# A hybrid decoder step on one core: groups of the down projection, order of the output projection's second half, and place of the gating functions

## The chip, the cores and the metric

The kernel runs on one core of one Trainium2 chip. The core has TensorE (PE, matmuls; PEld is its weight load), VectorE (DVE), ScalarE (ACT), GpSimd (POOL) and SyncE (SP), which issues most transfers. Each engine works off its own instruction stream in order; streams meet through semaphores. The metric is the device time of one execution in microseconds; less is better.

## The reference, cut to what matters

Two layers over 1024 prompt tokens and 8 decode tokens, 1032 columns in all, model width 1024, float32.

```python
mod = silu(c) @ w_ada + b_ada                       # shift1, scale1, gate1, shift2, scale2, gate2
h = rmsnorm(x, g_norm1) * (1 + scale1) + shift1
z, xbc, dt_raw, cq, ckv, kpe, u = split(h @ w_in)   # 384, 896, 6, 256, 128, 32, 256 columns
xbc = silu(causal_conv(xbc, conv_w, conv_b))        # x (384), B (256), C (256) of the scan
y = chunked_ssd_scan(x, dt, A, B, C)                # chunks of 128 tokens, decays exp(...)
ssd_out = rmsnorm((y + d_skip * x) * silu(z))       # two groups
mla_out = rmsnorm(latent_attention(...))            # 8 decode tokens read 64 pages each
pool_out = pool_mixer(u)
x = x + gate1 * (concat(ssd_out, mla_out, pool_out) @ w_out)
h2 = rmsnorm(x, g_norm2) * (1 + scale2) + shift2
x = x + gate2 * ((silu(h2 @ w_gate) * (h2 @ w_up)) @ w_down)   # FFN width 2816
```

## The kernel before

Activations lie transposed: 128 features on the partitions, the 1032 tokens along the free axis. Every large product is made from three matmuls on split operands: a value is cast to a short form (`wh`, `ac`, `op`, `X`; ScalarE, line 88) and the remainder (`wl` and the like) is the value less the cast one (line 93 on GpSimd in pieces of 129 columns, line 95 on VectorE); `mm3` (lines 139 to 141) adds high x high, low x high and high x low. A framework puts each engine's stream in order at compile time, by program order and by when it expects operands; `keep_in_program_order` pins an instruction behind the one written before it on its engine. Tiles come from pools of fixed size: 24 of kind C (`NA`), 20 of kind B (`NBUF`), seven accumulation banks `psd` and `psg`.

A layer goes through these stages.

- Norm, then input projection (`in_proj`): 16 blocks `m` of 128 output columns, three banks each. Each is evicted by VectorE (times the row's reciprocal norm `r`, line 291), the shift's contribution is copied (`sb`, line 292), the 8 decode columns are added (line 293), and ScalarE adds the bias in place (`evac`, line 296). Blocks 6 to 12 go through the causal convolution on VectorE (`conv`, `cv`), 13 to 15 are the gate z. From block 8 on, steps of the other mixers' preparation run in between (`side`): latents, decode queries, softplus, the pool mixer with its evictions `po` (line 436).
- `conv_silu` (line 383): ten Silu of 128x1032 on ScalarE, over the seven convolved blocks and the three of z, pinned behind each other. Then `table()` (line 213) loads ScalarE's function table with Ln and Exp, for all that follows.
- The weave: the chunked scan (decay products L517, matrices `M` L525 and `E`, L554 and L570 on the Silu's results), the latent attention and the decode tokens' pages, step by step in turn.
- Output projection (`out_proj`): two halves g of 516 columns, eight blocks m each. For step i = 8g + m the weight of i + 2 is loaded (`out_load`), that of i + 1 is split (`out_conv`; low part on VectorE for i in `OPV`). Each weight is loaded and split twice, once per half. A block's result times its gate plus the residual goes to `xb` (line 1440), is squared (`sq`, line 1446) and stored. Squares are added up by blocks; the sum over features is a matmul (line 1476), and `norm_half` makes the normalised operands X of one half during the other's products.
- FFN up (`ffn`, first part): 22 blocks f of 128, seven products each, results through Silu to DRAM (`actd`).
- FFN down (second part of `ffn`): the 22 activations go in groups `FFB`; for each group all eight output blocks m are computed, n x 3 x 3 matmuls of 344 columns for a group of n, and added to `x` (`resid`, lines 1356 to 1360, the last an addition over 8 columns on VectorE). An activation is loaded (`ar`) and split (`ac`, low part on GpSimd for even f, on VectorE for odd f) by `fetch`: the first group's before the first block, each later group's one per block from m = 1 of the group before. The weight of step i + 1 is split in step i, its low part on GpSimd.

Of the kernel before, what the change touches and what calls it, by code (L numbers as in the profile page):

```python
# [9 lines left out]
AF = mybir.ActivationFunctionType  # L10
ALU = mybir.AluOpType
# [6 lines left out]
TP = 1024  # L18
# [4 lines left out]
TQ, TQ2 = 258, 516  # L23
# [5 lines left out]
PAST = 8192  # L29
SCALE = 96 ** -0.5  # L30
FF = 22
FFB = (6, 6, 6, 4)
PGW = 258
GP = 16

# [13 lines left out]
class Net:  # L49
# [234 lines left out]
    def evac(self, o, ps, r, func=None):  # L284

        nc = self.nc
        n = T - 2 * TH
        b = self.S([128, 9], "sb", bufs=3)
        for t in range(3):
            a = slice(TH * t, min(TH * t + TH, T))  # L290
            nc.vector.tensor_tensor(out=o[:, a], in0=ps[t][:, :a.stop - a.start], in1=r[:, a], op=ALU.mult)  # L291
        nc.vector.tensor_copy(b, ps[2][:, n:n + 9])
        nc.vector.tensor_tensor(out=o[:, TP:], in0=o[:, TP:], in1=b[:, 1:9], op=ALU.add)
        if func is None:
            return b
        nc.scalar.activation(out=o[:, :TP], in_=o[:, :TP], func=func, bias=b[:, 0:1])

    def sums(self, parts, mix=False):

# [8 lines left out]
    def in_proj(self, l, X, r):  # L308
        nc, A = self.nc, self.A
        out = self.pj = {}  # L310
        raws = {} if l else {2: self.w2}
        W = {}
# [21 lines left out]
        for i, m in enumerate(ORD):  # L334
            if l or i:
                for j in range(1, WSA + 1):
                    prefetch(i + j)
                    conv(i + j)
                prefetch(i + WSA + 1)
            if i in pss:  # L340
                ps = pss.pop(i)
            else:
                ps = self.psum3(TH)
                self.gemm(ps, wk(i), X)
            del W[i]
            t = self.C(name=f"pj{m}")
            self.evac(t, ps, r, AF.Identity)
            out[m] = t
            if 6 <= m < 13:
                out[m] = self.conv(l, m - 6, t)  # L350
            yield
# [25 lines left out]
        nc.sync.dma_start(A["o_sconv"][l, :, c, 2, :], x[:, TP:])  # L377
        return y

    def conv_silu(self):  # L380
        for m in (9, 11, 6, 7, 8, 10, 12, 13, 14, 15):
            y = self.pj[m]
            self.tc.keep_in_program_order(self.nc.scalar.activation(out=y, in_=y, func=AF.Silu))

# [984 lines left out]
            yield  # L1369

    def out_load(self, l, i):
        if i < 16:
            self.oraw[i] = self.load_w(self.A["wout"][l, i % 8], 1024)

    def out_conv(self, i):
        if i < 16:
            self.ow[i] = self.split_w(self.oraw.pop(i), 1024, self.nc.vector if i in OPV else None)

    def out_pre(self, l):
# [15 lines left out]
    def out_proj(self, l, mod, xsrc, side):  # L1395


        nc, A = self.nc, self.A
        todo = [(g, m) for g in range(2) for m in range(8)]
        ms, W = self.ms, self.ow  # L1400
        self.xb, self.acc = [None, None], [None, None]
        for i, (g, m) in enumerate(todo):
            if m == 0:
                xb = self.xb[g] = {(e, j): self.C(name="xb") for e in range(2) for j in range(2)}
                sqs = self.acc[g] = [None, None, None]
            if m % 2 == 0:
                sq2 = self.C(name="sq")
            self.out_load(l, i + 2)
            self.out_conv(i + 1)
            if g:  # L1410
                for _ in range(SDO):
                    next(side[0], None)
            elif m == UF0:
                self.up_first(l)
            elif m > UF0:
                for _ in range(UFN):
                    self.up_ahead(l)
            if i == 1:
# [3 lines left out]
                for _ in self.out_cut(1):  # L1422
                    pass
                self.mx = self.om = None
            if m % 2 == 0:
                xt2 = self.C(name="xt")
            xt = xt2[:, TQ2 * (m % 2):TQ2 * (m % 2) + TQ2]
            nc.sync.dma_start(xt, xsrc(m)[:, TQ2 * g:TQ2 * g + TQ2])
            wh, wl = W.pop(i)
            ps = [self.bank()[:, :TQ] for _ in range(2)]  # L1430
            self.gemm(ps, lambda k: (wh[:, 128 * k:128 * k + 128], wl[:, 128 * k:128 * k + 128]),
                      [[o[:, TQ * j:TQ * j + TQ] for o in ms[g]] for j in range(2)])
            gt = mod[:, 16 + m, :]
            kp, e = divmod(m, 2)
            sq = sq2[:, TQ2 * (m % 2):TQ2 * (m % 2) + TQ2]
            for j in range(2):
                o = xb[e, j][:, TQ * kp:TQ * kp + TQ]
                a = slice(TQ * j, TQ * j + TQ)
# [6 lines left out]
                    nc.vector.tensor_tensor(out=o[:, n:], in0=xt[:, TQ2 - NB:], in1=t, op=ALU.add)  # L1445
                nc.scalar.activation(out=sq[:, a], in_=o, func=AF.Square)
                nc.sync.dma_start(A["xres"][m, :, TQ * (2 * g + j):TQ * (2 * g + j) + TQ], o)
            z = 2 if m == 7 else m % 2
            if sqs[z] is None:
                sqs[z] = sq  # L1450
            else:
                (nc.vector if g or m % 2 else nc.gpsimd).tensor_tensor(out=sqs[z], in0=sqs[z], in1=sq, op=ALU.add)
            if m == 7:
                del ms[g]
                yield

# [280 lines left out]
def build(nc, tc, A):  # L1737
    with tc.tile_pool(name="c", bufs=1) as cp, tc.tile_pool(name="s", bufs=1) as sm, \
# [54 lines left out]
        for l in range(L):  # L1793
# [13 lines left out]
            for m in range(16):  # L1807
                next(pr)
                if l == 0 and 4 + m < ADB[0][0][1]:
                    n.ada(l, mod, 4 + m)  # L1810
                if m >= 8:
                    next(side, None)
                if m == 11:
                    n.kt0 = []
                    for i in range(16):
                        n.smp_gather(l, 0, i, n.kt0)
            for _ in side:
                pass
            del X, r, pr
            n.conv_silu()  # L1820
            n.table()
            n.weave = Weave()
            n.wqk = {}
# [45 lines left out]
SDO = 2  # L1869
LD = 1  # L1870
KSP, SPV, KCV, OGV = (), (), 1, 0
UF0, UFN = 3, 2
WA0, W_L, W_F, W_G = 0, 10, 28, 30
OPO = (6, 7, 0, 1, 2, 3, 4, 5)
XFV, WPF, WPS, OPV = (), (), (), (0, 2, 4, 6, 8, 9, 10, 11, 12, 13, 14, 15)
# [165 lines left out]
```

## Time and profile before

| | |
|---|---|
| median of 3 runs | 3675.45 us (3671.54 to 3679.14) |
| the profiled execution: its time | 3681.19 us |
| its span, first to last instruction | 3679.3 us |
| its mean granted TensorE clock | 0.971 |

The profile is of one execution, which took 3681.19 us; 1.9 us of that lie outside the span. Times in the rows are counted from the span's start. Layer 0 has its input projection from about 68 to 267 us, its weave to about 1030, output projection to about 1148, FFN up to 1604 and FFN down to 1865; layer 1 begins there and has the same stages, the last input eviction at 2088, FFN down from 3416.

### The profile page before, as it was taken

To read this page: it belongs to the slowest core of one execution; us is meant where nothing else is said; L and a number is where in the kernel's file an instruction comes from. 1 tells how busy PE (TensorE), PEld (TensorE's weight loads), DVE (VectorE), ACT (ScalarE), POOL (GpSimd) and SP (SyncE) were. 2 spreads that over 40 slices of the span, in tenths; PEclk is the share of its full clock that TensorE was granted. 3 is DMA by queue.
4 is the path that set the end of the run, shared out by engine and by line. 5 is a ranking of instruction groups with operands and counts; after the bars stand their busy time and mean duration, and the time that the engine had idled before them with its cause. 6 is when DMAs were issued, how large, how long until landed. Compare 5 with 4: busy or idle time off the path is not lost. (4 is left out here: it accounts for less than half of the span.)

```text
span 3679.3 us, 68341 instructions
## 1 busy us (share of the span) xinstructions
PE 3441.4 (94%) x23682; PEld 3069.7 (83%) x23682; DVE 2237.4 (61%) x4328; ACT 1730.5 (47%) x4487; POOL 1867.1 (51%) x3346
## 2 busy tenths in 40 slices
PE   8988999898988999999999889899998889999999
PEld 6976666677887999999999676667777889999999
DVE  4557866767777555552345578767677675555432
ACT  4226566667755333331132456667677453333210
POOL 3336655555440766664433366556464226666642
PEclk9999999999999999999999999999999999999999
DMA  5233655443443222242222346444443522221531
GB/s 198 49 83 122 215 163 163 139 138 114 145 139 100 87 81 79 78 172 86 83 81 56 89 135 225 138 135 123 112 126 114 163 84 87 75 82 70 179 98 70
DMA packets 255336, 430.20 MB, mean 117 GB/s; under 512 B 38736, under 2 KB 180944, under 8 KB 254992
## 3 DMA queue, kind: packets, MB, share of 16 engines
q1 hardware_dynamic: 246800, 409.04, 35.0%
q0 software_dynamic: 8192, 16.79, 1.7%
q8 instruction: 189, 3.10, 0.3%
q14 instruction: 155, 1.27, 0.1%
HBM read 372.84 MB, written 52.87 MB: 116 GB/s over the span
## 5 line engine op out<-in xcount | busy, mean ns | idle before, releaser
L1165 POOL TENSOR_TENSOR lt<-pg,lt 128x128 fp32r<-128x128 f32 x1024 | 436.8, 460 | 465.1 <-ACT lt L1163 393.3
L1182 ACT ACTIVATE sqk<-psd 128x384 f32<-128x384 f32 x1024 | 498.6, 510 | 224.5 <-PE psd L141 152.8
L1329 DVE TENSOR_REDUCE ss<-sqk 128x12 f32<-128x768 f32 x448 | 422.4, 947 | 187.6 <-ACT sqk L1182 177.2
L139 PE MATMUL psd<-mv,lt 128*128 128x390 f32 x1024 | 436.1, 426 | 28.3 <-ACT scr L1183 25.1
L140 PE MATMUL psd<-X,wp 128*128 128x258 f32 x1408 | 398.8, 283 | 4.2 <-DVE wp L95 4.2
L139 PE MATMUL psd<-X,wp 128*128 128x258 f32 x1408 | 399.2, 284 | 3.5 <-ACT wp L88 3.5
L141 PE MATMUL psd<-X,wp 128*128 128x258 f32 x1408 | 398.1, 283 | 0.0
L140 PE MATMUL psd<-mv,lt 128*128 128x390 f32 x1024 | 361.5, 353 | 2.5 <-issue 2.2
L141 PE MATMUL psd<-mv,lt 128*128 128x390 f32 x1024 | 362.2, 354 | 1.1 <-issue 0.7
L93 POOL TENSOR_TENSOR wl<-wr,wh 128x129 fp32r<-128x129 f32 (+1 forms) x312 | 174.7, 598 | 311.6 <-ACT wh L88 244.8
L93 POOL TENSOR_TENSOR wp<-wr,wp 128x129 fp32r<-128x129 f32 x480 | 263.9, 581 | 103.0 <-ACT wp L88 99.1
L1116 POOL DMA_INDIRECT kp<-kpeT,kidx x256 | 260.1, 1016 | 105.4 <-issue 79.6
L140 PE MATMUL psg<-X,wp 128*128 128x258 f32 x1056 | 299.2, 283 | 7.1 <-DVE wp L95 7.1
L139 PEld LDWEIGHTS psd<-mv,lt 128*128 128x128 f32 x1024 | 200.2, 195 | 124.3 <-ACT scr L1183 55.2
L139 PE MATMUL psg<-X,wp 128*128 128x258 f32 x1056 | 299.1, 283 | 2.6 <-ACT wp L88 2.6
L141 PE MATMUL psg<-X,wp 128*128 128x258 f32 x1056 | 298.7, 283 | 0.0
L139 PE MATMUL psd<-op,wh 128*128 128x348 f32 (+1 forms) x792 | 250.9, 318 | 22.9 <-DVE pj L291 10.3
L140 PEld LDWEIGHTS psd<-X,wp 128*128 128x128 f32 x1408 | 267.0, 190 | 5.3 <-DVE wp L95 5.2
L139 PEld LDWEIGHTS psd<-X,wp 128*128 128x128 f32 x1408 | 266.9, 190 | 4.6 <-ACT wp L88 4.6
L141 PEld LDWEIGHTS psd<-X,wp 128*128 128x128 f32 x1408 | 267.0, 190 | 0.0
L140 PE MATMUL psd<-op,wl 128*128 128x348 f32 (+1 forms) x792 | 250.5, 316 | 7.0 <-POOL wl L93 3.5
L141 PE MATMUL psd<-op,wh 128*128 128x348 f32 (+1 forms) x792 | 248.3, 315 | 0.1
(467 smaller groups left out, 9870.3 us busy)
## 6 DMA issues: line engine op xcount, KB each, us to landing
pg<-pages SPq DMA_DIRECT2D x1024, 129.0 KB
wa<-wada SPq DMA_DIRECT2D x96, 512.0 KB
wr<-wff SPq DMA_DIRECT2D x96, 512.0 KB
ar<-actd SPq DMA_DIRECT2D x44, 516.0 KB
actd<-G SPq DMA_DIRECT2D x40, 516.0 KB
wd<-wdn SPq DMA_DIRECT2D x48, 384.0 KB
wr<-win SPq DMA_DIRECT2D x32, 512.0 KB
wr<-wout SPq DMA_DIRECT2D x32, 512.0 KB
```

Source lines behind the costliest of these rows:

```text
L93: nc.gpsimd.tensor_tensor(out=l[:, c], in0=x[:, c], in1=h[:, c].bitcast(F32), op=ALU.subtract)
L139: nc.tensor.matmul(ps, wh, xh, start=start, stop=False)
L140: nc.tensor.matmul(ps, wl, xh, start=False, stop=False)
L141: nc.tensor.matmul(ps, wh, xl, start=False, stop=stop)
L1116: self.nc.gpsimd.indirect_dma_start(out=kts[-1][:, 128 * g:128 * g + 128], out_offset=None, in_=self.A["kpeT"], in_offset=bass.IndirectOff ...
L1165: nc.gpsimd.tensor_tensor(out=ll[:, a], in0=v[:, a], in1=lh[:, a].bitcast(F32), op=ALU.subtract)
L1182: nc.scalar.activation(out=sq, in_=d[:, kc], func=AF.Square)
L1329: nc.vector.tensor_reduce(out=o, in_=x, axis=AX.X, op=ALU.add)
```

## The change

Three edits. The down projection's groups become 4, 6, 6, 6 instead of 6, 6, 6, 4. The output projection's second half goes through the blocks backwards, 7 to 0, and its first `ORE` = 2 blocks (7 and 6) take the split weights of the first half, which are kept for them. And the Silu of blocks 6 to 11 stands in the program behind block 12 of the input projection, that of block 12 behind block 13 (`SIL`), while blocks 13 to 15 are evicted with Silu in place of Identity, with a second Silu over the 8 decode columns, both pinned in program order.

```diff
--- before.py
+++ after.py
@@ -29,7 +29,7 @@
 PAST = 8192
 SCALE = 96 ** -0.5
 FF = 22
-FFB = (6, 6, 6, 4)
+FFB = (4, 6, 6, 6)
 PGW = 258
 GP = 16
 
@@ -293,7 +293,10 @@
         nc.vector.tensor_tensor(out=o[:, TP:], in0=o[:, TP:], in1=b[:, 1:9], op=ALU.add)
         if func is None:
             return b
-        nc.scalar.activation(out=o[:, :TP], in_=o[:, :TP], func=func, bias=b[:, 0:1])
+        keep = self.tc.keep_in_program_order if func == AF.Silu else lambda x: x
+        keep(nc.scalar.activation(out=o[:, :TP], in_=o[:, :TP], func=func, bias=b[:, 0:1]))
+        if func == AF.Silu:
+            keep(nc.scalar.activation(out=o[:, TP:], in_=o[:, TP:], func=func))
 
     def sums(self, parts, mix=False):
 
@@ -344,7 +347,7 @@
                 self.gemm(ps, wk(i), X)
             del W[i]
             t = self.C(name=f"pj{m}")
-            self.evac(t, ps, r, AF.Identity)
+            self.evac(t, ps, r, AF.Silu if m >= 13 else AF.Identity)
             out[m] = t
             if 6 <= m < 13:
                 out[m] = self.conv(l, m - 6, t)
@@ -377,8 +380,8 @@
         nc.sync.dma_start(A["o_sconv"][l, :, c, 2, :], x[:, TP:])
         return y
 
-    def conv_silu(self):
-        for m in (9, 11, 6, 7, 8, 10, 12, 13, 14, 15):
+    def conv_silu(self, ms):
+        for m in ms:
             y = self.pj[m]
             self.tc.keep_in_program_order(self.nc.scalar.activation(out=y, in_=y, func=AF.Silu))
 
@@ -1369,11 +1372,13 @@
             yield
 
     def out_load(self, l, i):
-        if i < 16:
-            self.oraw[i] = self.load_w(self.A["wout"][l, i % 8], 1024)
+        if i < 16 and not 8 <= i < 8 + ORE:
+            self.oraw[i] = self.load_w(self.A["wout"][l, i if i < 8 else 15 - i], 1024)
 
     def out_conv(self, i):
-        if i < 16:
+        if 8 <= i < 8 + ORE:
+            self.ow[i] = self.ow[15 - i]
+        elif i < 16:
             self.ow[i] = self.split_w(self.oraw.pop(i), 1024, self.nc.vector if i in OPV else None)
 
     def out_pre(self, l):
@@ -1396,23 +1401,24 @@
 
 
         nc, A = self.nc, self.A
-        todo = [(g, m) for g in range(2) for m in range(8)]
+
+        todo = [(g, q, 7 - q if g else q) for g in range(2) for q in range(8)]
         ms, W = self.ms, self.ow
         self.xb, self.acc = [None, None], [None, None]
-        for i, (g, m) in enumerate(todo):
-            if m == 0:
+        for i, (g, q, m) in enumerate(todo):
+            if q == 0:
                 xb = self.xb[g] = {(e, j): self.C(name="xb") for e in range(2) for j in range(2)}
                 sqs = self.acc[g] = [None, None, None]
-            if m % 2 == 0:
+            if q % 2 == 0:
                 sq2 = self.C(name="sq")
             self.out_load(l, i + 2)
             self.out_conv(i + 1)
             if g:
                 for _ in range(SDO):
                     next(side[0], None)
-            elif m == UF0:
+            elif q == UF0:
                 self.up_first(l)
-            elif m > UF0:
+            elif q > UF0:
                 for _ in range(UFN):
                     self.up_ahead(l)
             if i == 1:
@@ -1422,17 +1428,19 @@
                 for _ in self.out_cut(1):
                     pass
                 self.mx = self.om = None
-            if m % 2 == 0:
+            if q % 2 == 0:
                 xt2 = self.C(name="xt")
-            xt = xt2[:, TQ2 * (m % 2):TQ2 * (m % 2) + TQ2]
+            xt = xt2[:, TQ2 * (q % 2):TQ2 * (q % 2) + TQ2]
             nc.sync.dma_start(xt, xsrc(m)[:, TQ2 * g:TQ2 * g + TQ2])
-            wh, wl = W.pop(i)
+            wh, wl = W[i] if 8 - ORE <= i < 8 else W.pop(i)
+            if i >= 8:
+                W.pop(15 - i, None)
             ps = [self.bank()[:, :TQ] for _ in range(2)]
             self.gemm(ps, lambda k: (wh[:, 128 * k:128 * k + 128], wl[:, 128 * k:128 * k + 128]),
                       [[o[:, TQ * j:TQ * j + TQ] for o in ms[g]] for j in range(2)])
             gt = mod[:, 16 + m, :]
             kp, e = divmod(m, 2)
-            sq = sq2[:, TQ2 * (m % 2):TQ2 * (m % 2) + TQ2]
+            sq = sq2[:, TQ2 * (q % 2):TQ2 * (q % 2) + TQ2]
             for j in range(2):
                 o = xb[e, j][:, TQ * kp:TQ * kp + TQ]
                 a = slice(TQ * j, TQ * j + TQ)
@@ -1445,12 +1453,12 @@
                     nc.vector.tensor_tensor(out=o[:, n:], in0=xt[:, TQ2 - NB:], in1=t, op=ALU.add)
                 nc.scalar.activation(out=sq[:, a], in_=o, func=AF.Square)
                 nc.sync.dma_start(A["xres"][m, :, TQ * (2 * g + j):TQ * (2 * g + j) + TQ], o)
-            z = 2 if m == 7 else m % 2
+            z = 2 if q == 7 else q % 2
             if sqs[z] is None:
                 sqs[z] = sq
             else:
-                (nc.vector if g or m % 2 else nc.gpsimd).tensor_tensor(out=sqs[z], in0=sqs[z], in1=sq, op=ALU.add)
-            if m == 7:
+                (nc.vector if g or q % 2 else nc.gpsimd).tensor_tensor(out=sqs[z], in0=sqs[z], in1=sq, op=ALU.add)
+            if q == 7:
                 del ms[g]
                 yield
 
@@ -1810,6 +1818,8 @@
                     n.ada(l, mod, 4 + m)
                 if m >= 8:
                     next(side, None)
+                if m in SIL:
+                    n.conv_silu(SIL[m])
                 if m == 11:
                     n.kt0 = []
                     for i in range(16):
@@ -1817,7 +1827,6 @@
             for _ in side:
                 pass
             del X, r, pr
-            n.conv_silu()
             n.table()
             n.weave = Weave()
             n.wqk = {}
@@ -1869,7 +1878,8 @@
 SDO = 2
 LD = 1
 KSP, SPV, KCV, OGV = (), (), 1, 0
-UF0, UFN = 3, 2
+UF0, UFN, ORE = 3, 2, 2
+SIL = {12: (6, 7, 8, 9, 10, 11), 13: (12,)}
 WA0, W_L, W_F, W_G = 0, 10, 28, 30
 OPO = (6, 7, 0, 1, 2, 3, 4, 5)
 XFV, WPF, WPS, OPV = (), (), (), (0, 2, 4, 6, 8, 9, 10, 11, 12, 13, 14, 15)
```

## Rows read from the trace of the kernel before

**Rows 1.** The page, busy time of each engine: us, share of the span, instructions.
```profile
PE 3441.4 (94%) x23682; PEld 3069.7 (83%) x23682; DVE 2237.4 (61%) x4328; ACT 1730.5 (47%) x4487; POOL 1867.1 (51%) x3346
```

**Rows 2.** Windows: busy us (instructions) per engine, granted clock, DMA share, GB/s.
```profile
267.10:280.30 13.20, 5.43 (x25) 3.59 (x21) 1.06 (x4) 13.15 (x17) 0.00 (x0) 0.79 0.75 209
1604.50:1672.00 67.50, 62.30 (x369) 60.49 (x368) 33.33 (x40) 16.61 (x18) 44.88 (x97) 0.95 0.57 200
1800.00:1860.00 60.00, 60.00 (x383) 60.00 (x382) 26.52 (x66) 15.88 (x21) 20.60 (x39) 1.00 0.24 86
2089.40:2102.50 13.10, 5.47 (x25) 3.59 (x21) 1.11 (x4) 13.05 (x17) 0.00 (x0) 0.81 0.70 192
```

**Rows 3.** Timeline of ScalarE behind layer 0's last eviction: start, us, instruction [idle before].
```profile
266.00 1.15 ACT L296 ACTIVATE pj<-pj,sb 128x1024 f32<-128x1024 f32 x1 [0.25 <-DVE sb L292]
267.17 1.28 ACT L383 ACT_TABLE_LOAD   x1
268.46 6.78 ACT L383 ACTIVATE cv<-cv 128x1032 f32<-128x1032 f32 x7
275.15 2.95 ACT L383 ACTIVATE pj<-pj 128x1032 f32<-128x1032 f32 x3
278.11 1.28 ACT L213 ACT_TABLE_LOAD   x1
279.40 0.89 ACT L525 ACTIVATE M<-psg,nat 128x128 f32<-128x128 f32 x3
```

**Rows 4.** Timeline of TensorE, same place.
```profile
280.34 2.93 PE L517 MATMUL psg<-acr,kt 128*128 128x128 f32 x12 [3.04 <-ACT M L525]
```

**Rows 5.** Timeline of ScalarE, end of the output projection's first half, layer 0.
```profile
1086.49 1.04 ACT L88 CAST wh<-wr 128x1024 fp32r<-128x1024 f32 x1 [0.99 <-DMA wr<-wout]
1087.44 0.41 ACT L1446 ACTIVATE sq<-xb 128x258 f32<-128x258 f32 x1
```

**Rows 6.** Timeline of ScalarE, evictions of blocks 12 to 14, layer 0.
```profile
232.41 1.15 ACT L296 ACTIVATE pj<-pj,sb 128x1024 f32<-128x1024 f32 x1 [8.94 <-DVE sb L292]
241.23 1.05 ACT L88 CAST wh<-wr 128x1024 fp32r<-128x1024 f32 x1 [7.68 <-PE psg L140]
...
251.51 2.02 ACT L436 ACTIVATE po<-psg,vt 128x344 f32<-128x344 f32 x4
```

**Rows 7.** Timeline of TensorE, into the output projection's second half, layer 0.
```profile
1087.90 0.70 PE L1476 MATMUL psd<-sq,kt 128*128 128x258 f32 x2 [1.00 <-ACT sq L1446]
...
1101.33 0.39 PE L140 MATMUL psg<-op,wl 128*128 128x258 f32 x1 [1.01 <-DVE wl L95]
```

**Rows 8.** Timeline of VectorE, same place.
```profile
1083.28 1.57 DVE L95 TENSOR_TENSOR wl<-wr,wh 128x1024 fp32r<-128x1024 f32 x1 [0.90 <-ACT wh L88]
...
1087.58 1.22 DVE L95 TENSOR_TENSOR wl<-wr,wh 128x1024 fp32r<-128x1024 f32 x1
```

**Rows 9.** Timeline of TensorE, start of the down projection, layer 1.
```profile
3424.90 0.42 PE L139 MATMUL psd<-ac,wh 128*128 128x344 f32 x1 [1.32 <-ACT ac L88]
...
3430.04 0.42 PE L141 MATMUL psd<-ac,wh 128*128 128x344 f32 x1 [1.14 <-POOL ac L93]
...
3450.63 0.40 PE L139 MATMUL psd<-ac,wh 128*128 128x344 f32 x1 [0.95 <-DVE x L1356]
```

**Rows 10.** Timeline of GpSimd, same place.
```profile
3426.38 4.46 POOL L93 TENSOR_TENSOR ac<-ar,ac 128x129 fp32r<-128x129 f32 x8 [3.27 <-ACT ac L88]
...
3439.30 5.11 POOL L93 TENSOR_TENSOR wl<-wd,wh 128x129 fp32r<-128x129 f32 x12
```

**Rows 11.** Timeline of VectorE, same place.
```profile
3424.88 1.23 DVE L95 TENSOR_TENSOR ac<-ar,ac 128x1032 fp32r<-128x1032 f32 x1 [4.64 <-ACT ac L88]
3428.02 1.23 DVE L95 TENSOR_TENSOR ac<-ar,ac 128x1032 fp32r<-128x1032 f32 x1 [1.91 <-ACT ac L88]
3433.86 1.06 DVE L1356 SCALAR_TENSOR_TENSOR x<-psd,mod,x 128x344 f32<-128x344 f32 x2 [4.61 <-PE psd L141]
...
3435.49 14.50 DVE L1360 TENSOR_TENSOR x<-x,rs 128x8 f32<-128x8 f32 x1
```

## The prediction

> **What bounds the kernel now.** Three views, in this order. First the page's busy times: TensorE is busy 94% of the span [rows 1], so a change pays only where TensorE stands still or runs at a lower clock, and an edit that takes work from another engine pays only where TensorE waits for that engine. Next the windows around the edited code [rows 2]. In the 13.2 us behind the last input projection of layer 0, TensorE is busy 5.43 us and ScalarE 13.15 us, and the granted clock is 0.79; layer 1 shows the same (13.1, 5.47, 13.05; 0.81). In the first 67.5 us of the down projection TensorE has 62.30 us. In its last group it has all 60.00 of 60 us, 383 matmuls, which also gives the price of one 344-column matmul: 60.00 / 383 = 0.157 us. Then the timelines, which say what each stall waits for.
>
> **Gating functions during the input projection (the largest part).** After block 15's eviction [rows 3] ScalarE loads Silu's table (1.28), runs ten Silu of 128x1032 (6.78 for seven, 2.95 for three), loads the table with Ln and Exp back (1.28), and only then, at 279.40, makes the first decay matrix. From 267.17 to 279.40 are 12.23 us. TensorE's next decay products wait for that matrix until 280.34 [rows 4]. After the change seven Silu (blocks 6 to 12) stand earlier and three are the evictions themselves (Silu in the place of Identity, on the same 1024 columns), each with a second one over eight columns; per layer that is three large ScalarE instructions less, three tiny ones more, and two table loads as before. Behind block 15 remain the tiny one (I take 0.2 us, an estimate from the 0.41 us that 258 columns cost in [rows 5], less most of the columns) and one table load, 1.28. So ScalarE is free 12.23 - 1.5 = 10.7 us earlier; that is the upper bound.
>
> What hides the moved work: six Silu and the table load go behind block 12's eviction, 1.28 + 6 x 0.97 = 7.1 us. There ScalarE idles from 233.56 (232.41 + 1.15) to 241.23, 7.7 us [rows 6]; the cast behind the gap waits for TensorE to free its tile. It fits with 0.6 us to spare; without that cover the cast of block 15's weight would be late by the excess. The seventh (block 12) comes behind block 13's eviction, where the pool mixer's evictions (251.51) release banks to TensorE. It is queued ahead of them: about 1.0 us, with the tiny ones 1.3 us, that block 15's products start later. No queue is passed: no DMA moves.
>
> What the 10.7 us are worth: in that window TensorE stands still 13.2 - 5.43 = 7.8 us and 13.1 - 5.47 = 7.6 us [rows 2]; the products it does there have still to be done, in its order, ahead of the decay products. So I take the idle time, not ScalarE's burst: 7.7 - 1.3 = 6.4, and about 1.1 for running the 5.43 us at the full instead of 0.79 of the clock (5.43 x 0.21): 7.5 per layer, **-15.0** for two. Bounds: -21.4 (the whole burst), and -6 if the weave behind gives half of it back, because its next waits (page loads, VectorE's reductions) are met earlier.
>
> **Output projection's second half backwards.** Blocks 7 and 6 use the split weights that the first half has just used. Per layer this drops two loads of 512 KB from SP's queue, two casts on ScalarE and two subtractions on VectorE, and moves nothing ahead of another queue. Tiles: the two kept pairs stand where the pairs of blocks 8 and 9 stood, so no other load gets a tile earlier. The place is the end of the first half. The cast for block 9 (1.04, itself 0.99 late for its load) runs ahead of the last square [rows 5]; TensorE's row sums wait for that square 1.00 us [rows 7]. VectorE spends 1.57 and 1.22 us on the two subtractions [rows 8], and the statistics of the first half stand directly behind the second; in that queue comes block 10's subtraction, for which TensorE waits 1.01 us at 1101.33 [rows 7]. VectorE being 2.8 us ahead, both waits should go: 1.0 + 1.0 = 2.0 per layer, **-4.0**. Bounds: 0 if other work on the two queues moves into the gap, and -7.6 (1.0 + 2.8 per layer) if every later conversion comes as much earlier. The reversed order of loads of x and of stores costs nothing: the same transfers, read by nobody before the down projection; a late x load would stall VectorE's residual first.
>
> **Groups of 4, 6, 6, 6.** The number of matmuls, loads of activations, splits and evictions stays; so does that of the weights' loads. What moves is which group comes first. Now the first block needs six activations, and these come late: in layer 1 TensorE waits at 3424.90 for the fourth (1.32) and at 3430.04 for the fifth (1.14) [rows 9], which GpSimd splits from 3426.38 for 4.46 us [rows 10]; the first residual is at 3433.86 [rows 11]. With four, the last one needed is the fourth, split by VectorE at 3424.88 + 1.23; its remaining products end by about 3426.8. The old block has 18 matmuls more, 18 x 0.157 = 2.8 us, so at equal work it stood at 3431.0: gain 4.2, less about 0.6 for the second block's weight, whose split can only start when the fourth cast is done: 3.6 per layer.
>
> Against it: at 3435.49 VectorE starts an 8-column addition and is held 14.50 us [rows 11], while GpSimd runs splits without a gap (12 pieces in 5.11 us, 0.43 each, in [rows 10]). TensorE lives on free banks and stops at 3450.63 for 0.95 us [rows 9], so 14.2 us after the addition began. Two blocks pass in that time, and each is now 18 x 0.157 = 2.8 us shorter: it would stop after 14.2 - 5.7 = 8.5 us. A hold of 14.5 would then cost 6.0 us, none if it is under 8.5. GpSimd's run is shorter too (four pieces per weight, not six; 44 pieces, not 54) and the fifth activation no longer stands ahead of the weights; I take 2.6, near the middle. Net -1.0 per layer, **-2.0**. Bounds: -11.4 (layer 0, whose stalls were longer, and no hold) and +7.2 (a full hold, 6.0, with 1.2 for a lower clock after it). The last group grows to six; TensorE has no idle time there [rows 2], and the three evictions behind the last matmul are the same: 0.
>
> [...]
>
> **Sum.** -15.0 - 4.0 - 2.0 = -21.0 us against the profiled execution's own 3681.19: 3660.2, a ratio of 0.9943. That execution is 5.7 us above the median of the three runs; the ratio on 3675.45 gives **3654 us**. Differences below 0.2% (7.4 us) can't be told from none here.
>
> **Rivals.**
> (1) The forecast: chance 0.60, its own range 3645 to 3662.
> (2) VectorE gets through at the next piece and the whole ScalarE burst counts. For: the split at 3428.02 ran its plain 1.23 us amid GpSimd's own; against, in the same group, the addition that was held [rows 11]. Without the hold 5.2 us are gained, and up to 6.4 more from the burst: 3643 to 3649. Chance 0.15. [...]
> (3) The hold in the shorter group is as long as now: each layer loses 6.0 + 1.2 - 3.6 = 3.6 instead of gaining 1.0: 9.2 more, 3663. For: GpSimd's queue still runs ahead as far as tiles allow. Chance 0.12.
> (4) The Silu do not pay: the weave is limited elsewhere (page transfers, VectorE) or the pinned Silu push a cast or an eviction late, so the 15 us are given back. Left are 6.0 us: 3669, no difference to be told. For: VectorE and GpSimd are busy 61% and 51% of the whole span [rows 1], so other waits stand close behind; against: in the window itself VectorE has 1.06 us of work and GpSimd none [rows 2]. Chance 0.08.
> (5) Slower: the hold repeats. If VectorE is held not at one residual but at each of the first three of the short group, the odd activations' splits, also VectorE's, come late as well, and the second group starts without them. One hold as long as now costs 7.2 past the 8.5 us of cover; two more have no cover, 14.5 each: 36 per layer, less 3.6, 65 for both; 19.0 gained elsewhere leave +46: 3721. It decides once the two layers lose over 27 us together. Against: now it happens once per layer. Chance 0.05.
>
> Faster: (1), (2) and most of (3): 0.83. Same: (4) and the rest: 0.12. Slower 0.05. The range that leaves out 2 in 10: from the middle of (2) with some of the part bounds, 3638, to (4), 3668.
>
> **What would show it.** Right: two Silu tables loaded as before, but the first behind block 12's eviction; the first decay matrix some 10 us closer behind block 15's eviction and the window's granted clock higher; row sums without a wait for the square; the first residual of the down projection about 7 us after the fourth activation's cast. Wrong: block 15's products starting later than 1.5 us against block 14's; more than two table loads per layer; a VectorE addition held over 8.5 us in the first group with TensorE stopped for a bank; a weave as much longer as the window is shorter.

## The result, and the profile after

The changed kernel takes 3628.86 us (median of 4 runs, 3626.76 to 3641.6), the kernel before 3673.49 beside it (4 runs): ratio 0.9886, 95% interval 0.9863 to 0.9908. Two later comparisons gave 0.9901 (0.9884 to 0.9918) and 0.9870 (0.9838 to 0.9901). The change saves 36 to 47 us; the forecast was 21, and 3628.86 lies below its range (3638 to 3668). One execution of all3 and one of no_o below took 5420.9 and 4179.4 us at a mean clock of 0.555 and 0.744, and the ratios leave them out.

The profile after is of an execution of 3626.76 us, span 3624.7. Its busy times, to be held against [rows 1]:

```profile
PE 3417.8 (94%) x23682; PEld 3054.4 (84%) x23682; DVE 2205.4 (61%) x4324; ACT 1726.6 (48%) x4483; POOL 1863.4 (51%) x3346
```

TensorE does the same 23682 matmuls in 23.6 us less busy time: its clock was higher (0.980 in the mean, from 0.971), which the forecast had all but left out.

**Gating functions.** ScalarE's timeline in layer 0, from block 12's eviction on; it answers to [rows 3, 6]:

```profile
233.48 1.15 ACT L297 ACTIVATE pj<-pj,sb 128x1024 f32<-128x1024 f32 x1 [8.95 <-DVE sb L292]
234.65 1.28 ACT L386 ACT_TABLE_LOAD   x1
235.95 5.85 ACT L386 ACTIVATE cv<-cv 128x1032 f32<-128x1032 f32 x6
242.29 1.05 ACT L88 CAST wh<-wr 128x1024 fp32r<-128x1024 f32 x1 [0.49 <-issue]
...
250.67 1.05 ACT L386 ACTIVATE cv<-cv 128x1032 f32<-128x1032 f32 x1
251.62 1.13 ACT L297 ACTIVATE pj<-pj,sb 128x1024 f32<-128x1024 f32 x1
...
265.93 1.15 ACT L297 ACTIVATE pj<-pj,sb 128x1024 f32<-128x1024 f32 x1 [3.13 <-DVE sb L292]
266.98 0.20 ACT L299 ACTIVATE pj<-pj 128x8 f32<-128x8 f32 x1
267.20 1.28 ACT L213 ACT_TABLE_LOAD   x1
268.49 0.16 ACT L523 COPY ex<-psg 128x3 f32<-128x3 f32 x1
268.55 0.89 ACT L528 ACTIVATE M<-psg,nat 128x128 f32<-128x128 f32 x3
```

Table load and six Silu fill the gap behind block 12 as foreseen. Block 15's eviction begins at 265.93, in [rows 3] at 266.00: the moved Silu cost no time there (over the 13 profiles below that have this part whole or not at all, the means are 265.6 with it and 265.8 without). The first decay matrix starts 2.6 us behind that eviction's start in place of 13.4, in both layers.

What that is worth to TensorE is read from two windows from the last eviction's end to the first product on `kps`. Each holds 64 matmuls, 60 of them on the same operands in both (in the changed kernel four products on `cv` come ahead of the window and four on `kp` inside it). First before (TensorE's wait, its work behind the wait, both), then after. Columns as in [rows 2].

```profile
267.15:280.34 13.19, 5.38 (x25) 3.59 (x22) 1.01 (x4) 13.14 (x17) 0.00 (x0) 0.79 0.75 208
280.34:288.46 8.12, 8.12 (x39) 5.60 (x40) 5.19 (x16) 6.36 (x18) 6.53 (x15) 0.72 0.01 2
267.15:288.46 21.31, 13.49 (x64) 9.20 (x61) 6.20 (x20) 19.50 (x34) 6.53 (x15) 0.76 0.47 130
```
```profile
267.08:277.78 10.70, 10.70 (x64) 6.46 (x59) 5.38 (x18) 8.23 (x23) 5.01 (x12) 1.00 0.81 208
```

21.31 us became 10.70, so 10.6 us: 7.8 of idle time and 2.8 because nearly the same matmuls run at a granted clock of 1.00 in place of 0.76. Most of the 2.8 lies behind the stall, where 39 matmuls had 0.72 of the clock without a wait between them (8.12 x 0.28 = 2.3, an estimate from that window). Layer 1 gives 21.5 and 10.7, at 0.76 and 1.00, and 39 matmuls behind the stall there take 8.35 us at 0.70, again without a wait. In the eight kernels below with the whole gating part the first decay matrix comes 2.6 or 2.7 us behind the eviction too, in both layers.

**Down projection.** The first stretch of layer 0, which answers to the second row of [rows 2], and what TensorE waits for in the first 65 us of layer 1, before and after:

```profile
1582.80:1650.30 67.50, 64.73 (x406) 63.59 (x406) 32.09 (x58) 18.10 (x21) 50.47 (x108) 1.00 0.63 215
```
```profile
PE psd L141 <- POOL ac L93: 1.6, 2, 1.1
PE psd L139 <- ACT ac L88: 1.3, 1, 1.3
PE psd L141 <- DVE ac L95: 1.1, 1, 1.1
PE psd L139 <- DVE x L1356: 1.0, 1, 1.0
```
```profile
PE psd L141 <- DVE ac L95: 1.1, 1, 1.1
PE psd L139 <- ACT ac L88: 0.7, 1, 0.7
PE psd L141 <- POOL ac L93: 0.7, 1, 0.7
```

In 67.5 us TensorE now does 406 matmuls, not 369: idle time fell from 5.2 to 2.8 us and the clock is 1.00 in place of 0.95. The wait for the residual (`x`, L1356) is gone. VectorE is still held, but elsewhere; its timeline and GpSimd's in layer 1:

```profile
3382.51 0.50 DVE L1363 TENSOR_TENSOR x<-x,rs 128x8 f32<-128x8 f32 x1
...
3387.99 7.55 DVE L95 TENSOR_TENSOR ac<-ar,ac 128x1032 fp32r<-128x1032 f32 x1
```
```profile
3380.82 3.45 POOL L93 TENSOR_TENSOR ac<-ar,ac 128x129 fp32r<-128x129 f32 x8 [1.94 <-ACT ac L88]
3384.23 3.44 POOL L93 TENSOR_TENSOR wl<-wd,wh 128x129 fp32r<-128x129 f32 x8
3387.62 3.45 POOL L93 TENSOR_TENSOR ac<-ar,ac 128x129 fp32r<-128x129 f32 x8
3391.03 3.42 POOL L93 TENSOR_TENSOR wl<-wd,wh 128x129 fp32r<-128x129 f32 x8
```

A split that took 1.23 us elsewhere [rows 11] takes 7.55 and ends 1.1 us after GpSimd's run without a gap (3391.03 + 3.42). TensorE does not wait for it.

**Output projection.** Lines of TensorE with a wait, second half of layer 0, before and after. The forecast counted the 1.0 us at 1087.90 and the 1.01 at 1101.33 [rows 7]; the longest one, behind them, it had not counted:

```profile
1116.56 0.39 PE L139 MATMUL psg<-op,wh 128*128 128x258 f32 x1 [1.41 <-ACT wh L88]
1120.12 0.58 PE L139 MATMUL psd<-op,wh 128*128 128x258 f32 x1 [3.05 <-ACT wh L88]
```
```profile
1081.36 0.39 PE L140 MATMUL psg<-op,wl 128*128 128x258 f32 x1 [1.02 <-DVE wl L95]
...
1096.38 0.39 PE L139 MATMUL psg<-op,wh 128*128 128x258 f32 x1 [1.02 <-ACT wh L88]
1097.64 0.39 PE L140 MATMUL psg<-op,wl 128*128 128x258 f32 x1 [0.75 <-DVE wl L95]
```

No wait of over 1.02 us for a cast (`wh`) is left in layer 0; in layer 1 one of 3.37 went the same way, and the longest left is 1.69. Of the two waits that the forecast meant to remove, the one of the row sums is gone in layer 0 and fell from 1.38 to 0.86 us in layer 1. The one for `wl` at 1101.33 is still there, at 1081.36.

**The weave.** It isn't edited, and yet in this pair of profiles it is shorter: 761.0 to 753.0 us in layer 0 and 746.1 to 741.7 in layer 1 (first decay matrix to first square). The experiments tell whether that is the change's.

### The profile page after: what moved, and what is told of

Its sections match the earlier page's. It is cut to its first block, busy times and chain, and to the rows that moved or that the text cites. A ratio compares the mean times of both kernels' runs of the same rounds, so it can differ in the third digit from the quotient of the medians.

```text
span 3624.7 us, 68321 instructions
## 1 busy us (share of the span) xinstructions
PE 3417.8 (94%) x23682; PEld 3054.4 (84%) x23682; DVE 2205.4 (61%) x4324; ACT 1726.6 (48%) x4483; POOL 1863.4 (51%) x3346
## 4 chain that ended last, share of the span: by engine, by line
PE 70%; DVE 10%; ACT 4%; issue 2%; DMA 2%; another core or an unknown queue 1%; POOL 1%; SPq 0%; ACTq 0%; DVEq 0%; POOLq 0%
PE psd L139 13%; PE psd L141 12%; PE psd L140 12%; PE psg L140 6%; PE psg L139 6%; PE psg L141 6%; PE psg L922 2%; DVE ss L1332 2%; PE psm L1232 2%; PE psm L192 1%; PE psg L840 1%; PE psm L1137 1%; ACT sqk L1185 1%; PE psg L945 1%; ACT xb L1502 1%
## 5 line engine op out<-in xcount | busy, mean ns | idle before, releaser
L1119 POOL DMA_INDIRECT kp<-kpeT,kidx x256 | 259.3, 1013 | 101.4 <-issue 78.8
L139 PE MATMUL psd<-op,wh 128*128 128x348 f32 (+1 forms) x792 | 249.8, 316 | 19.2 <-DVE pj L291 10.3
```

Source lines behind the costliest of these rows:

```text
L139: nc.tensor.matmul(ps, wh, xh, start=start, stop=False)
L1119: self.nc.gpsimd.indirect_dma_start(out=kts[-1][:, 128 * g:128 * g + 128], out_offset=None, in_=self.A["kpeT"], in_offset=bass.IndirectOff ...
```

## The experiments

Three kernels with one part each, and one with half of the gating part.

```diff
 g_only: before with
-FFB = (6, 6, 6, 4)
+FFB = (4, 6, 6, 6)
 o_only: before with the edits of out_load, out_conv and out_proj (ORE = 2)
 s_only: before with the edits of evac, in_proj and conv_silu (SIL)
 s_half: s_only with
-SIL = {12: (6, 7, 8, 9, 10, 11), 13: (12,)}
+SIL = {15: (9, 11, 6, 7, 8, 10, 12)}
```

**g_only.** 

> The kernel before with the groups 4, 6, 6, 6 alone. By the prediction's term (3.6 us won per layer, 2.6 lost to VectorE held at the 8-column addition): -2 us, ratio 0.9995, a held addition of about 14.5 us still there, TensorE's clock in the first 65 us of the down projection as before (0.95 and 0.97). By the theory that the profile after suggests (no residual is held, 2.4 to 2.8 us less idle, and with the shorter stalls the clock stays at 1.00, worth 62.3 x 0.05 and 58.3 x 0.03 us): -5.5 and -4.6, together about -10, ratio 0.9973. The weaves (first decay matrix to first square, 761.0 and 746.0 us) aren't touched: if they differ by more than 2 us here, that is what the same weave varies by from execution to execution, and the 7.9 and 4.3 us that they were shorter in the profile after need no other cause.

Measured: 0.9972 (0.9961 to 0.9983), 10.3 us of 3681.5. The down projections (first product to last addition) take 254.4 and 253.8 us (260.6 and 258.8 before), the clock in their first 65 us is 1.00, and no residual is held; a split is, 7.60 and 7.47 us, and nobody waits for it. The second theory holds, the prediction's term doesn't. The weave of layer 0, whose instructions come in the same order on all engines as before, took 754.1 us.

**o_only.** 

> The kernel before with the output projection's second half backwards and its two kept weights alone. By the prediction's term (two stalls of 1.0 us gone per layer): -4 us, ratio 0.9989, the stage at 104.7 and 109.4 us. By the theory that a stall costs its idle time and a lower clock behind it as well: -9 us, ratio 0.9975, the stage at 102.6 and 106.3 us as in the profile after, with the granted clock 0.97 and 0.95 in place of 0.95 and 0.92. If kept weights also keep tiles that later stages want, FFN up (456.0 us) gets longer by 1 us, as it did in the profile after.

Measured: 0.9979 (0.9970 to 0.9988), 7.7 us. The stage (first square to last) takes 104.5 and 103.2 us, the waits of 3.05 and 3.37 us are gone, and FFN up is 2.0 and 1.4 us longer. That the kept tiles are why FFN up is longer isn't shown.

**s_only.** 

> The kernel before with the gating functions moved alone. By the prediction's term (6.4 us of idle time and 1.1 of clock per layer): -15 us, ratio 0.9959, the first decay matrix 9.4 us closer behind block 15's eviction, of which some is given back. By the theory that the whole burst counts (idle 7.8, the lower clock in the window 1.1 and behind it about 2, nothing given back): -21.6, ratio 0.9941. By the theory that the weave too is shorter because of this part (7.9 and 4.3 us in the profile after): -34, ratio 0.9908. Block 15's eviction stays where it was (266.0 us) in the last two.

Measured: 0.9943 (0.9929 to 0.9956), 21.0 us: the whole burst. The first decay matrix comes 2.6 us behind the eviction in both layers. The weaves take 758.0 and 742.8 us, in an execution of 3648.83 us, 10.5 below the median.

**s_half.** 

> Only half of the gating part: blocks 13 to 15 are evicted with Silu, the seven convolved blocks keep their place behind block 15. ScalarE's burst there is 0.2 + 6.78 + 1.28 = 8.3 us in place of 12.2, so the first decay matrix comes 3.9 us earlier in each layer. If every microsecond of the burst counts once, and the clock with it: -8 to -10 us, ratio 0.9975. If TensorE's products in that window (5.4 us) hide part of it: by the share of the prediction's term, 3.9 / 10.7 of -15, so -5.5 us, ratio 0.9985. If the weave's gain hangs on where ScalarE's Silu stand and not on the length of the burst, the weave is shorter by more than 2 us per layer as well.

Measured: 0.9953 (0.9939 to 0.9966), 17.3 us, more than either expected. The decay matrix comes 9.3 us behind the eviction in both layers, 4.1 earlier, as ScalarE's timeline says:

```profile
264.65 1.15 ACT L297 ACTIVATE pj<-pj,sb 128x1024 f32<-128x1024 f32 x1 [2.26 <-DVE sb L292]
265.71 0.19 ACT L299 ACTIVATE pj<-pj 128x8 f32<-128x8 f32 x1
265.81 6.77 ACT L386 ACTIVATE cv<-cv 128x1032 f32<-128x1032 f32 x7
272.60 1.28 ACT L213 ACT_TABLE_LOAD   x1
```

That is 8.2 us for two layers. Its time beyond that is not explained by this place, and stays open; the weaves (753.2 and 745.7) are within what they vary by (below). By the times alone half of the part (interval 12.5 to 22.5 us) can't be told from the whole one: that the gain goes with the length of ScalarE's burst is read from the profiles.

Next, two that take an edit apart, and two that go further than the change.

```diff
 o_rev: o_only with
-UF0, UFN, ORE = 3, 2, 2
+UF0, UFN, ORE = 3, 2, 0
 h_only: before, in resid, with
-        t = self.S([128, NB], "rs", bufs=2)
-        nc.vector.tensor_tensor(out=t, in0=ps[2][:, n:], in1=g[:, 1:9], op=ALU.mult)
-        nc.vector.tensor_tensor(out=x[:, TP:], in0=x[:, TP:], in1=t, op=ALU.add)
+        nc.vector.tensor_tensor(out=ps[2][:, n:], in0=ps[2][:, n:], in1=g[:, 1:9], op=ALU.mult)
+        nc.vector.tensor_tensor(out=x[:, TP:], in0=x[:, TP:], in1=ps[2][:, n:], op=ALU.add)
 a_3667: the changed kernel with FFB = (3, 6, 6, 7)
 a_ore4: the changed kernel with ORE = 4
```

**o_rev.** 

> The kernel before with the output projection's second half backwards, but every weight loaded and split again: the order alone, without the kept weights. By the prediction the order costs and brings nothing, since the same transfers run: ratio 1.000, and TensorE's two long waits for a cast in the second half (1.4 and 3.1 us in layer 0, 1.4 and 3.4 in layer 1) are there as before. If the order itself brought part of the 7.7 us of the kernel with both (0.9979): 0.999.

Measured: 1.0021 (1.0007 to 1.0034), the stage at 105.9 and 111.1 us, with the waits for a cast as before (3.1 and 3.2 us the longest). The kept weights bring the gain, not the order. Why the time is 0.2% above that of before is open. One stretch of its profile stands out, layer 1's input projection, which this edit doesn't touch: 225.9 us from the last residual to block 15's eviction, against 219.0 to 223.2 us in the other 13 profiles so far; whether the edit has to do with it isn't shown.

**h_only.** 

> The kernel before, groups 6, 6, 6, 4, with one edit: the 8-column addition to the residual reads its second operand from the accumulation bank, not from SBUF. By the prediction's reading, that VectorE is held because two SBUF operands have to get past GpSimd's stream, the additions of 11.7 and 14.5 us fall to under 0.6 us, or the next VectorE instruction with two SBUF operands is held in their place. What it brings: by the theory that the hold costs only what TensorE waits for it (nothing in layer 0, 0.95 us in layer 1), 1 to 2 us, ratio 0.9996, and the waits for the first block's activations stay. By the rival that the hold, and not the shorter first block, is where the group change's 10 us came from: ratio 0.9973.

Measured: 1.0021 (1.0011 to 1.0031). All 64 additions are now short, and the hold went on to a split, 2.27 us in layer 0 and this in layer 1 (first the additions, duration in ns lowest/median/highest, then VectorE's timeline):

```profile
L1359 DVE TENSOR_TENSOR x<-x,psg x64: 152/161/165, 1614.5 to 3657.7; 128x8 f32<-128x8 f32 x64
```
```profile
3428.07 5.02 DVE L95 TENSOR_TENSOR ac<-ar,ac 128x1032 fp32r<-128x1032 f32 x1
```

The down projections take 258.8 and 259.3 us, as with the hold (258.0 to 260.6 in six others with these groups). So the held residual cost TensorE next to nothing, and the group change's gain isn't its removal. The 64 additions, with one operand in SBUF and one in the bank, took 0.165 us at most, also those at 3419.68, 3425.50 and 3434.29, inside a run of GpSimd's without a gap (3414.90 to 3436.56); with both in SBUF, the first of each layer was held 11.74 and 14.50 us in the kernel before. The rows of the prediction show a hold beside GpSimd's run and no more; that the number of SBUF operands goes with it is first seen here. That the time is 0.2% longer stays open here too.

**a_3667.** 

> The changed kernel with groups of 3, 6, 6, 7 in place of 4, 6, 6, 6. By the theory that the first block's wait for its activations is what the groups change, the wait for the fourth cast (1.0 and 0.7 us) goes as well: 1 to 2 us less over both layers, 0.9882 against the kernel before. By the prediction's rule of cover, the first two blocks are now 27 matmuls shorter than with six, 4.2 us each, so that TensorE stops for a bank once VectorE is held more than 14.2 - 8.5 = 5.7 us; a hold of 7.5 as in the changed kernel costs 1.8 us per layer and shows as a wait of TensorE for the residual: 0.9892.

Measured: 0.9909 (0.9894 to 0.9924). The wait for the fourth cast is gone; what is left of TensorE's waits in layer 1 is this:

```profile
PE psd L141 <- DVE ac L95: 1.2, 1, 1.2
PE psd L141 <- POOL ac L93: 0.4, 1, 0.4
```

The down projections take 253.4 and 252.5 us, 0.9 and 1.2 less than the mean with 4, 6, 6, 6; in the time that can't be seen, and the ratio lies above both expectations. The addition was held 6.3 us in both layers, past the 5.7 of the prediction's rule, and TensorE did not stop for it: the rule is too strict by at least 0.6 us.

**a_ore4.** 

> The changed kernel with four kept weights in the output projection (blocks 7, 6, 5 and 4) in place of two. By the theory that each conversion that is left out takes a wait for a cast with it (0.9 to 1.0 us each in the second half of the profile after), 2 us less per layer: 0.9876 against the kernel before. By the theory that the two conversions at the end of the first half were the harmful ones, nothing more: 0.9886. By the rival that four more of the 24 tiles held through the first half delay the loads of weights and of FFN up: slower than the changed kernel by some us, 0.989 to 0.991.

Measured: 0.9912 (0.9898 to 0.9926); the stage takes 107.2 and 108.4 us, more than with two kept weights. The first weight that is loaded after the kept ones now comes late, as TensorE's waits show (the first two of the second half, layer 0):

```profile
1098.16 0.58 PE L139 MATMUL psg<-op,wh 128*128 128x258 f32 x1 [5.15 <-ACT wh L88]
1101.11 0.58 PE L140 MATMUL psg<-op,wl 128*128 128x258 f32 x1 [2.15 <-DVE wl L95]
```

Last, the changed kernel and three that each lack one of its parts, on one chip (no_g with `FFB = (6, 6, 6, 4)`, no_o with the output projection of before, no_s with the gating functions of before).

**all3.** 

> The changed kernel once more, beside three that each lack one part, on the same chip. The chips of the earlier comparisons differ (the kernel before took 3673, 3681 and 3665 us in them). If the parts' gains are the same everywhere: ratio 0.9886 to 0.9894. If part of the first comparison's gain was that chip's own: 0.990 to 0.992.

**no_g.** 

> The changed kernel with the groups 6, 6, 6, 4 of before. If the parts add up and the groups are worth 10.3 us as alone: 0.0028 above the changed kernel. By the prediction's 2 us: 0.0005 above it. The down projections take 258 to 260 us in place of 254, with a residual held 11 us or more, and TensorE's clock is under 1.00 in their first 65 us.

**no_o.** 

> The changed kernel with the output projection of before. Alone, that part was worth 7.7 us: 0.0021 above the changed kernel if the parts add up, 0.0011 by the prediction's 4 us. By the theory that its gain was two waits for a cast in the second half (3.1 and 3.4 us) and not the end of the first half: those waits are there again, and the stage takes 106 to 111 us in place of 103 to 108.

**no_s.** 

> The changed kernel with the gating functions where they were. If this part is worth 10.8 us per layer wherever it stands: 0.0058 above the changed kernel, the first decay matrix 13.4 us behind block 15's eviction in place of 2.6, TensorE's granted clock under 0.8 between them. By the prediction's 15 us: 0.0041 above it.

Measured: all3 0.9901 (0.9884 to 0.9918, so it doesn't decide between its two expectations), no_g 0.9940 (0.9925 to 0.9956), no_o 0.9925 (0.9906 to 0.9944), no_s 0.9948 (0.9931 to 0.9965), of 3660.15 us. The parts add up within their uncertainty (all3 itself saves 36.2 us):

| us | predicted | alone | missing from all three | stages, 13 profiles so far |
|---|---|---|---|---|
| gating functions | 15.0 | 21.0 | 17.2 | 21.6 |
| output projection | 4.0 | 7.7 | 8.8 | 8.8, less 1.9 in FFN up |
| groups | 2.0 | 10.3 | 14.3 | 11.2 |
| sum | 21.0 | 39.0 | 40.3 | 39.7 |

A single one of the third column is uncertain by some 9 us (two intervals of 0.0015 to 0.0019 each way). The last column is the surest: differences of the mean stage lengths of both layers, for the gating functions of the time from block 15's eviction to the first decay matrix (in each row one of the 14 profiles so far is left out, s_half, a_ore4 or a_3667, which has the part in a third form). Without kept weights (7 profiles) the output projection took 105.9 to 111.0 us in layer 0 and 109.2 to 111.4 in layer 1, with two (6 profiles) 100.9 to 104.5 and 103.2 to 107.7; means 107.4 and 110.4 against 103.2 and 105.8. FFN up was 456.3 and 456.4 against 457.5 and 457.2. The down projection took 258.0 to 260.6 with six first (7 profiles) and 253.1 to 254.6 with four (6 profiles); means 260.2 and 259.0 against 254.3 and 253.7. The longest wait for a cast in the output projection was 2.9 to 3.4 us in all 14 layers without kept weights, and at most 1.7 in the 12 with two.

**The weave** took 750.7 to 761.0 us in layer 0 and 738.0 to 748.4 in layer 1 over the 14 profiles so far. With the gating part whole its means are 753.8 and 743.2, without it 755.0 and 744.7. The 761.0 of the profile before is the longest of the 14: most of the 8.0 us were this execution's, and the weave gives nothing of the gating part's gain back.

One point was open after these: why two kept weights take away the wait for a later cast, that of step 13. In the kernel before, TensorE's order has the first matmul of step 13 ahead of 46 matmuls of step 12; with two kept weights it hasn't. So TensorE's order alone was changed.

```diff
 o_ord: before (a_ord: the changed kernel) with
+        a = nc.tensor.matmul(ps, wh, xh, start=start, stop=False)
+        if keep and start:
+            self.tc.keep_in_program_order(a)
 (likewise the last of an accumulation; in out_proj, keep=i >= 12)
```

**o_ord.** 

> The kernel before, with TensorE's order alone changed in the output projection: from block 12 of the 16 steps on, the first and last matmul of each accumulation are pinned in program order. In the kernel before, the framework has put the first matmul of step 13, which needs that step's cast, ahead of 46 matmuls of step 12 that are ready, and likewise that of step 15 ahead of 46 of step 14; no other engine's order changes here, and all weights are loaded and split twice as before. If the output projection's gain in the changed kernel is that the first of these places went away with the two kept weights: the waits of 3.1 and 3.4 us are gone, and those of 0.9 us at step 15 too, the stage takes 103 to 106 us, ratio 0.9975 (3.0 to 3.4 and 0.9 us per layer and some clock). If the gain is that casts and subtractions are left out: the waits move to the next cast, ratio 1.000.

**a_ord.** 

> The changed kernel with the same pins. Only the place at step 15 is left there (waits of 0.9 and 1.7 us in the profile after): 1 to 2 us per layer less than the changed kernel, 0.0005 to 0.001 lower in ratio, if those products find nothing else to wait for. If the wait only moves: the same as the changed kernel.

**after_b.** 

> The changed kernel on the same chip as the two before it, for comparison: 0.9886 to 0.9901 by the two earlier comparisons.

Measured: o_ord 0.9983 (0.9964 to 1.0002), a_ord 0.9875 (0.9841 to 0.9908), after_b 0.9870 (0.9838 to 0.9901), of 3591.37 us. o_ord's interval holds both of its expected ratios, so its stage decides: it takes 110.8 and 110.4 us, and the wait has only moved from step 13's cast to step 12's low part (3.2 and 3.0 us). The order alone is not the cause. TensorE's two waits in layer 0, and VectorE up to that low part:

```profile
1072.58 0.39 PE L140 MATMUL psg<-op,wh 128*128 128x258 f32 x1 [1.18 <-ACT wh L88]
1076.14 0.58 PE L143 MATMUL psg<-op,wl 128*128 128x258 f32 x1 [3.18 <-DVE wl L95]
```
```profile
1072.51 1.22 DVE L95 TENSOR_TENSOR X<-xb,X 128x1032 fp32r<-128x1032 f32 x1
1073.65 0.16 DVE L1450 TENSOR_TENSOR xb<-xt,rs 128x8 f32<-128x8 f32 x1
1073.73 1.23 DVE L1515 TENSOR_TENSOR xb<-xb,xb 128x1032 f32<-128x1032 f32 x1
1074.87 1.22 DVE L95 TENSOR_TENSOR wl<-wr,wh 128x1024 fp32r<-128x1024 f32 x1
```

VectorE has no idle time between these: step 12's low part stands behind the operands `X` of the first half. It is so in the kernel before as well. ScalarE's casts of steps 12 and 13 there, VectorE's low part of step 12 there, and the same low part in the changed kernel:

```profile
1115.47 1.03 ACT L88 CAST wh<-wr 128x1024 fp32r<-128x1024 f32 x1
...
1119.02 1.04 ACT L88 CAST wh<-wr 128x1024 fp32r<-128x1024 f32 x1 [0.92 <-DMA wr<-wout]
```
```profile
1118.71 1.22 DVE L95 TENSOR_TENSOR wl<-wr,wh 128x1024 fp32r<-128x1024 f32 x1
```
```profile
1096.36 1.23 DVE L95 TENSOR_TENSOR wl<-wr,wh 128x1024 fp32r<-128x1024 f32 x1 [0.20 <-ACT wh L88]
```

Before, the low part starts 2.2 us behind the end of its cast (1115.47 + 1.03). In the changed kernel VectorE is idle 0.20 us until that cast is done and starts at once, and TensorE waits 0.75 us for the low part (1097.64 above). The cast of step 13 waits 0.92 us for its weight, whose load SP issued at 1115.10, behind stores of VectorE's results. So VectorE was late, and with two kept weights it is not; o_rev, which lacks only them, has the waits. That the two dropped subtractions, 2.8 us [rows 8], make the difference, and not the dropped casts or loads, is argued from their place: they stand ahead of that same work in VectorE's queue. a_ord is as fast as after_b, so the order brings nothing in the changed kernel either.

## Why the prediction was wrong, point by point

The direction and each place were right, and each size was too small: a stall of TensorE was priced by its idle time alone, at the output projection the wrong waits were counted, and at the groups a hold was charged that cost nothing.

**Gating functions**: forecast 15.0, measured 21.6 in the stages. The cover behind block 12 held and the table loads went as said. Two steps failed. "So I take the idle time, not ScalarE's burst": 64 matmuls, nearly the same, took 13.49 us busy before and 10.70 after; the prediction took 1.1 us of clock inside the window and none for the 8.12 us behind it at 0.72. And "1.3 us that block 15's products start later": the eviction came at 265.93, against 266.00 before. The upper bound, 21.4, was the answer, and rival (2) had this half right.

**Output projection**: forecast 4.0, measured 8.8 in the stage, 6.9 with FFN up. "Both waits should go" failed in the choice of waits: the one for `wl` stayed, at 1.02 us. What went is a wait of 3.0 to 3.4 us per layer for a later cast. The step's bound of 7.6, that every later conversion comes earlier, had the mechanism; the value was taken from the two waits that stood next to the edit. VectorE's delay reaches further: at step 12 it is still 2.2 us.

**Groups**: forecast 2.0, measured 11.2 in the stages. "I take 2.6" for the hold failed: VectorE was held 4.4 to 7.7 us in the six kernels with four first, on a split and not on the residual, under the 8.5 us that the prediction had itself worked out as free, and TensorE never waited for it; even the holds of 11.5 to 14.8 us with six first cost at most 1.3 us. And 3.6 per layer was idle time alone: the idle time fell by 2.4 and 2.8 us, and the clock, back at 1.00 from 0.95 and 0.97, gave 62.3 x 0.05 = 3.1 and 59.8 x 0.03 = 1.8 more (estimates from the busy time and the clock before). The 1.2 us for a lower clock in the bound of +7.2 and in rivals (3) and (5) stands on no row, and no run shows it: the longest wait for a held residual was 1.3 us. The sign "about 7 us after the fourth activation's cast" doesn't fit the working above it (3426.8, 2.0 us behind that cast's end); after, the first residual starts 1.8 us behind it in both layers.

**Rivals**: (2) came nearest in time and was wrong on its first half, since VectorE did not get through at the next piece (7.55 us against 0.43). (3) and (5) needed a hold that TensorE waits for; (4) a weave that gives the gain back. None of these came.

## What to carry to other kernels

Price a stall of TensorE by the time that the same matmuls take from before it to well behind it; here the clock added a third to the idle time at one place (2.8 to 7.8 us) and nearly as much again at another (an estimated 4.9 to 5.2, both layers of the down projection). Before an edit upstream in a chain of loads, casts and products is costed, list all waits of the stage and begin with the longest: it need not stand beside the edit. And look at a stage that the edit doesn't touch in several profiles before explaining why it got shorter.

## What was not expected of the hardware

A VectorE instruction with two SBUF operands that was held while GpSimd ran without a gap (11.5 to 14.8 us on the residual with six first, 4.4 to 7.7 on a split with four) passed its hold on in h_only, where it lost one of those operands: the next such instruction, a split, took 2.27 and 5.02 us in place of 1.23. Not every one is held: in the changed kernel the addition at 3382.51 got through in 0.50 us inside a run of GpSimd's (3380.82 to 3394.45). What decides that is open.

The kernel before took medians of 3660, 3665, 3673 and 3681 us in four comparisons and 3591 in the last, on a chip that had given 3681. The weave holds the difference: in the three profiles of the last comparison, and unedited, it took 714.0 to 715.5 us in layer 0 and 703.0 to 712.5 in layer 1, in the others 750.7 to 761.0 and 738.0 to 748.4, while FFN up stayed at 456 to 458. Why is open.
